# A two-layer hybrid attention trunk on one core: the last 512 output columns cut at 384 in place of 256, their last sum of squares on VectorE, and another list of issue

## The chip, the core and the metric

The kernel runs on one core of one Trainium2 chip. The metric is the device time of one execution in microseconds (us); three runs of the kernel before took 294.9, 294.93 and 295.31 us, median 294.93 us. A core has five engines, each of which executes its own instructions in the order in which they were put into its queue: TensorE (PE: matrix products; PEld is its loading of the stationary operand), VectorE (DVE), ScalarE (ACT), GpSimd (POOL) and SyncE (SP, which here only starts transfers). The engines wait for each other by semaphores. SBUF is the memory on the core, 128 partitions wide; PSUM is the memory in 8 banks into which TensorE writes.

## The reference

The input x is one sequence of 256 tokens with D = 1024 features, in 32-bit floats. Two layers follow one another, and a last normalization:

```
c_act = silu(c)
for layer in range(2):
    shift, scale, gate = split(c_act @ w_ada[layer] + b_ada[layer], 3)
    h = rms_norm(x, norm_g[layer]) * (1 + scale) + shift
    if layer == 0: y = even_mixer(h, ...)   # projections, attention A and B, w_out_even
    else:          y = odd_mixer(h, ...)    # projections, attention C, w_out_odd
    x = x + gate * y
return rms_norm(x, final_g)     # x * rsqrt(mean(x*x) + eps) * final_g
```

The even layer has two groups of 8 heads. Group A attends to a sliding window of 128 tokens with a learned sink for each head. Group B has three branches (compressed, selected and sliding window), each with a gate. The odd layer has 16 heads with causal attention in blocks of 256, which at 256 tokens is plain causal attention. In both, a SiLU path multiplies the heads' output before one output projection of 1024 x 1024.

## The kernel before, in words

**Products in three parts.** A 32-bit product is made of three products in a faster type. Each weight tile `raw` is split into a rounded part `whi` (a copy by ScalarE) and a remainder `wlo` (a subtraction by VectorE), each activation into `hhi`, `hlo` or `ghi`, `glo`, and `mm3` (L567) issues hi x hi, hi x lo and lo x hi into one bank. In the output projections the tokens are stationary, 128 at a time, and up to 512 weight columns stream past them: 8 slices of the inner dimension times 3 parts, 24 matmuls for 128 tokens and one bank. Each of these matmuls loads its own 128 x 128 stationary operand.

**Tokens.** The 256 tokens lie as two halves `t` = 0 and 1 of 128 partitions; `xs` (128 x 2 x 1024) holds the running x.

**Attention.** `quad_probs` (L1023) handles four heads. TensorE writes the scores into four banks; for each head VectorE adds the mask and takes the minimum (`tensor_tensor_reduce`), ScalarE takes the exponential, VectorE the reciprocal of the sum; the multiplication by it is split between VectorE and ScalarE. Then TensorE transposes the head's probabilities, tile `sm`, in three matmuls of 128 columns with the identity (a part of the tile `ta`) into the bank `ps_pt`, of which there is one, and ScalarE copies the bank into `pT`:

```
L37    BANKS = {"pj": 3, "s": 2, "pt": 1, "o": 1, "m": 1}
...
            pt = bank("pt")
            for n in range(3):
                T.transpose(pt[:, n * P : (n + 1) * P], sms[j][:, n * P : (n + 1) * P], ident)
            pT = sb([P, 3 * P], "pT", 4)
            A.copy(pT, pt[:, : 3 * P])
```

`quad_values` and `b_half` (L1102) then multiply `pT` with the values into the bank `ps_o`. In the traces `sm_125` to `sm_129` are the five buffers of `sm`, and slices of `bigA` serve as further ones.

**The junction.** The even layer's last attention is the second `b_half`; its output projection `out_proj` (L1179 to L1192) comes next. Since the projection's first products need only heads that are finished, its matmuls (`ps_pj` from `whi`, `wlo` and `ghi`, `glo`, 512 columns) stand in TensorE's queue between the transposes of that last attention. Between them stand the conditioning's small products for the odd layer (bank `ps_m`; `acc` is their sum, made by VectorE).

**The end.** The odd layer's output projection (L1244 to L1279) runs by halves of 512 output columns `n`. In the second half the gate is multiplied into the raw weights first, so that the product can be added to `xs` without it. Within a half the work goes by pieces, each a bank of its own: token half 0 with 512 columns, then token half 1, which for n = 1 is in two pieces of 256 columns (L1259). `plan.fence("pe")` keeps TensorE's pieces in this order. After each piece `add_scaled` (L377) adds the bank to `xs` on VectorE and sums the squares of those columns, then VectorE multiplies them by the final weights `fg` into `ot` (a view of the tile `oT`). The square goes to ScalarE, whose sum goes to a column of `parts`; GpSimd adds the sums of a token half's earlier pieces into another column of it. After the last piece of a token half ScalarE takes the root of the sum (with the earlier pieces' sum as its bias), VectorE the reciprocal, and ScalarE scales columns 0 to 320 (`CUT`) of `ot` and VectorE the other 704; a transfer of each follows.

**What sets the order.** Nothing is issued while the program above runs: every call is recorded by `Plan` (L178 to L260) with the earlier calls it depends on. At the end `Plan.issue` goes through the table `ORDER` (L38), 2985 numbers of recorded calls, and issues them in that order, each to its own engine's queue. The table can put any call anywhere as long as what it depends on stands ahead of it. Since all are issued from one line, every instruction of the trace has the line L252 (L253 in the changed kernel), and one tells them apart by their tiles.

The transfers of the weights go through SP's queue into five buffers `raw`; some small loads at the start go through ScalarE's and GpSimd's queues.

Of the kernel before, what the change touches and what calls it, by code (L numbers as in the profile page):

```python
# [38 lines left out]
0 4 74 8 10 3 5 11 2 12 9 6 13 1 14 15 7 77 16 17 34 18 35 59 75 79 22 19 76 36 20 60 78 38 61 80 39 30 42 62 63  # L39
21 64 37 65 81 66 67 69 70 44 45 71 72 46 47 48 83 82 96 97 98 99 100 101 102 103 104 105 106 107 108 109 110  # L40
111 112 113 114 115 116 117 118 119 120 121 122 123 124 125 126 127 54 73 31 49 84 55 128 50 43 40 142 129 51 68
56 130 131 52 138 91 53 94 93 57 143 139 135 172 169 132 173 136 140 160 144 178 86 58 163 133 164 89 145 156
181 95 154 161 170 175 134 137 85 149 152 146 176 166 87 32 150 182 88 157 179 90 174 147 171 177 141 151 148
153 196 92 162 208 209 180 219 158 222 165 23 167 183 255 202 205 203 210 184 187 159 211 223 199 212 224 193
220 194 168 197 225 190 206 198 188 221 191 226 227 228 229 230 231 232 233 234 235 236 237 238 239 240 241 242
243 244 245 214 155 246 213 256 189 207 185 247 248 204 253 200 201 25 192 195 216 186 215 249 250 264 257 260
286 254 277 268 278 269 251 259 252 330 289 290 291 258 217 262 218 266 274 331 271 287 261 283 288 279 272 273
263 316 280 281 313 310 317 284 301 282 270 318 295 267 285 304 328 292 302 332 327 311 307 333 319 275 305 329
296 320 303 276 334 297 335 306 265 321 298 314 336 337 338 339 340 341 342 343 344 345 346 347 357 358 322 293
308 348 349 309 355 350 324 351 323 352 315 294 299 353 354 300 325 359 356 312 370 361 391 388 392 389 366 326  # L50
379 393 418 373 371 360 382 364 419 362 385 390 376 420 377 368 424 365 374 363 369 383 415 384 378 386 425 416
380 426 427 421 428 412 375 400 406 429 372 381 367 397 413 422 387 409 401 451 402 394 403 423 398 399 404 407
405 430 431 432 433 434 435 436 437 438 439 440 441 452 442 395 414 443 444 449 445 447 446 516 417 410 517 453
512 455 396 450 408 411 833 458 464 456 485 482 462 448 473 646 474 467 483 454 476 470 484 486 479 459 460 475
468 702 465 466 487 469 488 480 546 457 489 461 471 506 463 491 547 490 518 521 492 493 477 509 472 519 494 478
515 520 510 481 523 550 507 522 551 553 525 524 495 554 500 552 555 559 497 496 536 556 535 534 508 557 558 498
501 562 832 548 537 647 499 560 549 605 563 511 502 527 561 565 566 567 604 836 532 564 530 571 526 568 603 569
543 572 606 573 538 570 574 575 533 577 578 704 576 579 580 703 583 584 585 531 513 708 581 582 589 503 542 648
539 607 608 609 618 705 610 612 619 586 587 711 712 620 529 709 710 714 590 504 591 713 595 588 505 623 831 611
596 592 593 621 717 715 716 594 540 706 720 541 721 597 718 649 622 719 624 722 723 726 724 639 626 640 613 625  # L60
614 707 615 616 650 641 727 728 725 729 730 627 732 731 733 734 738 735 514 739 617 736 27 628 644 629 602 630
28 651 834 643 906 598 631 737 26 740 741 744 742 745 743 528 633 599 747 41 642 601 600 746 750 860 632 840 748
907 749 753 751 752 754 755 634 635 756 757 545 636 652 655 544 637 653 838 656 839 858 24 654 657 1057 835 658
638 758 759 760 761 762 763 764 765 766 767 768 769 770 771 772 773 776 782 837 778 777 783 843 844 842 841 847
848 846 845 851 852 850 849 855 856 854 853 659 784 786 1065 908 774 661 775 662 660 785 859 780 788 792 779 909
968 969 970 971 972 973 974 975 976 977 978 979 980 981 982 983 793 910 864 861 863 862 868 865 867 866 872 869
871 870 876 873 875 874 986 781 663 664 790 787 665 789 791 984 667 1066 668 666 994 995 990 991 877 794 996 670
29 795 671 878 992 797 985 803 879 796 912 998 880 881 798 1002 987 799 669 673 674 675 679 800 680 814 672 681
911 882 913 988 685 676 809 883 808 677 989 686 678 1000 682 884 1001 683 1067 801 687 691 802 1003 692 693 885
684 688 689 690 1068 886 694 804 805 697 914 695 806 698 696 887 807 699 1069 888 889 890 891 892 893 894 895  # L70
896 897 898 899 900 901 902 903 700 1132 1133 1134 1135 1136 1137 1138 1139 915 701 810 918 919 1070 904 999 921
815 920 997 811 812 1140 993 905 1004 1148 916 1071 924 922 925 1041 1042 1043 1044 926 813 1005 923 1142 930
1006 1255 927 928 816 817 1045 1013 929 1007 818 1256 933 1072 1146 931 932 819 1150 934 935 1012 939 1046 1047
1008 936 937 917 940 1048 1144 938 1257 1025 1049 941 1147 1141 942 945 1009 1010 943 946 947 944 951 1018 948
1050 949 950 1011 1262 1152 1051 1077 952 953 954 1014 1015 1258 1019 1016 1052 1143 1053 1154 955 957 958 1145
1259 1024 1054 1076 1078 1260 956 959 1153 1017 960 961 963 1149 964 1194 1195 1196 1197 1198 1199 1200 1201
1401 1020 1079 962 1208 965 1055 1210 1273 1151 966 1021 1261 1022 1056 967 1023 1058 1155 820 821 822 823 824
825 826 827 1156 1026 1211 1027 1028 1082 1059 1085 1209 1157 1029 1086 1159 1087 1091 1083 1092 1212 1080 1084
1093 1402 1060 1170 1088 1164 1061 1062 1171 1089 1090 1097 1094 1214 1098 1063 1095 1099 1263 1206 1064 1103
1202 1073 1216 1272 1104 1213 1158 1096 1165 1100 1105 1160 1264 1207 1204 1265 1161 1162 1163 1101 1102 1106  # L80
1107 1081 1205 1278 1279 1280 1281 1282 1283 1284 1285 1217 1166 1203 1266 1167 1215 645 1168 1108 1109 1176
1169 1438 1112 1292 1113 1114 1267 1118 1119 1110 1177 1172 828 1173 1218 1174 1290 1293 1175 1111 1268 1115
1030 1031 1032 1033 1034 1035 1036 1037 1219 1274 1178 1221 1179 1116 1180 1294 1117 1220 1120 1288 1226 1181
1121 1275 1124 1122 857 1222 1227 1233 1223 1125 1296 1300 1286 1224 1276 1298 1126 33 1123 1127 1225 1277 1128
1295 829 1437 1074 1075 1228 1229 1230 1289 1129 1130 1232 1340 1341 1342 1343 1344 1345 1346 1347 1403 1416
1269 1038 1231 1443 1234 1287 1444 1299 1239 1235 1404 1297 1238 1301 1270 1291 1236 1405 1182 1183 1184 1185
1186 1187 1188 1189 1190 1191 1192 1193 1237 1240 1241 1271 1242 1039 1480 1406 1407 1408 1409 1410 1302 1131
1243 1411 1303 1244 1245 1246 1247 1248 1249 1250 1251 1305 1360 1304 1494 1362 1481 1311 1412 830 1488 1363
1306 1310 1307 1495 1356 1308 1354 1482 1309 1352 1489 1490 1491 1316 1357 1492 1312 1322 1313 1314 1496 1317
1497 1417 1418 1483 1040 1350 1348 1315 1498 1499 1506 1493 1353 1318 1422 1358 1319 1446 1320 1419 1500 1252  # L90
1323 1321 1501 1355 1502 1503 1361 1359 1420 1507 1324 1508 1504 1509 1351 1349 1505 1364 1421 1510 1511 1365
1325 1414 1562 1566 1413 1366 1423 1567 1326 1327 1328 1329 1330 1331 1332 1333 1334 1335 1336 1337 1338 1339
1424 1372 1367 1379 1445 1253 1368 1369 1425 1373 1378 1384 1370 1598 1599 1426 1574 1575 1371 1484 1374 1375
1376 1576 1577 1377 1254 1447 1427 1600 1518 1380 1381 1382 1601 1512 1385 1602 1383 1578 1386 1387 1486 1388
1485 1563 1487 1389 1448 1462 1428 1429 1430 1431 1432 1390 1391 1392 1393 1394 1395 1396 1397 1433 1398 1439
1603 1564 1568 1579 1463 1399 1513 1519 1440 1434 1520 1580 1514 1521 1522 1515 1441 1565 1516 1604 1400 1569
1517 1524 1525 1523 1530 1581 1442 1531 1435 1465 1449 1464 1526 1582 1532 1436 1527 1605 1528 1606 1533 1529
1570 1607 1536 1583 1534 1584 1535 1450 1685 1571 1608 1451 1572 1585 1452 1586 1587 1554 1453 1454 1455 1456
1573 1588 1589 1686 1537 1609 1538 1590 1558 1457 1555 1591 1592 1593 1458 1594 1595 1596 1597 1559 1610 1611
1556 1622 1612 1613 1614 1689 1415 1459 1539 1615 1616 1560 1623 1557 1624 1690 1691 1628 1617 1460 1618 1619  # L100
1620 1629 1631 1621 1625 1630 1466 1467 1468 1469 1470 1471 1472 1473 1632 1633 1626 1634 1461 1635 1561 1474
# [1247 lines left out]
```

## Time and profile before

| | before |
|---|---|
| median of three runs | 294.93 us (294.9 to 295.31) |
| profiled execution, first to last instruction | 292.6 us |
| TensorE busy | 281.4 us (96%) |
| VectorE busy | 248.8 us (85%) |
| ScalarE busy | 196.4 us (67%) |
| GpSimd busy | 9.1 us (3%) |
| bytes moved | 71.70 MB, mean 245 GB/s |
| mean granted TensorE clock | 0.987 |

The profile is of one execution. Its span of 292.6 us runs from the first instruction to the last one; the median of the runs has 2.3 us more than that, which lie before and behind, so a span is compared with spans and a run with runs. The clock is the share of full speed that TensorE was granted. In the rows by instruction the columns are the start in us, the duration, the engine, the operation and what it writes and reads, and in brackets the wait before it and who ended it. In the rows by group they are the count, the busy time, the mean duration in ns and, behind the bar, the idle time of the engine ahead of the group. A matmul's duration in such a row is longer than its share of TensorE's time, since successive ones overlap: the pace is read from start to start.

### The profile page before, as it was taken

The page shows a single profiled execution, that of the slowest core. Times are in us where ns is not written, and L with a number is a line of the kernel's source. Part 1 is how long each engine was busy: PE and PEld are TensorE (multiplying, and loading weights), DVE is VectorE, ACT ScalarE, POOL GpSimd, SP SyncE. Part 2 cuts the span into 40 slices and gives each one's busy share as a digit, 9 for nine tenths or more (in the row PEclk, how much of TensorE's full clock was granted, in tenths as well). Part 3 has the DMA queues.
Part 4 walks back from the last instruction along what each step waited for, and adds up shares of the span by engine and source line. Part 5 has one row for each costly group of instructions (what it writes and reads, how often), then busy time and mean ns, then how long its engine had stood idle before and what let it go on. Part 6 is the DMA issues. An engine that isn't in the chain of part 4 may idle for free.

```text
span 292.6 us, 6200 instructions
## 1 busy us (share of the span) xinstructions
PE 281.4 (96%) x2292; PEld 242.6 (83%) x2292; DVE 248.8 (85%) x585; ACT 196.4 (67%) x465; POOL 9.1 (3%) x34
## 2 busy tenths in 40 slices
PE   6899999999999999999999999999999999999991
PEld 5778887999799887777768899998899989887890
DVE  0398898999999999999999659898938899899963
ACT  3586356586999999995289652665459358793831
POOL 3200000000000000000010000000000000000100
PEclk9799999999999999999999999999999999999997
DMA  7999999998898849857969968965094874402003
GB/s 241 374 390 382 376 388 380 327 333 253 276 343 264 281 131 331 288 203 241 273 206 349 350 221 276 333 228 171 15 338 154 296 280 146 143 2 72 1 2 143
DMA packets 62398, 71.70 MB, mean 245 GB/s; under 512 B 3416, under 2 KB 53024, under 8 KB 62368
## 3 DMA queue, kind: packets, MB, share of 16 engines
q1 hardware_dynamic: 61792, 70.84, 72.9%
q10 hardware_dynamic: 448, 0.41, 0.4%
q8 instruction: 18, 0.29, 0.4%
q14 instruction: 12, 0.10, 0.1%
q0 software_dynamic: 128, 0.05, 0.1%
HBM read 70.25 MB, written 1.05 MB: 244 GB/s over the span
## 4 chain that ended last, share of the span: by engine, by line
PE 87%; DVE 7%; DMA 2%; ACT 2%; issue 1%; POOL 0%; DVEq 0%; ACTq 0%; POOLq 0%
PE ps_pj L252 56%; PE ps_s L252 11%; PE ps_o L252 8%; PE ps_pt L252 7%; PE ps_m L252 5%; DMA rows<-in_norm_g_dram 2%; DVE acc L252 1%; DVE sm L252 1%; DVE bigA L252 1%; DVE t L252 1%; DVE oT L252 1%; DVE wlo L252 1%; ACT whi L252 1%; ACT sm L252 0%; ACT hhi L252 0%
## 5 line engine op out<-in xcount | busy, mean ns | idle before, releaser
L252 ACT CAST whi<-raw 128x1024 fp32r<-128x1024 f32 (+4 forms) x84 | 75.4, 915 | 43.2 <-PE ps_pj L252 20.4
L252 DVE TENSOR_TENSOR wlo<-raw,whi 128x1024 fp32r<-128x1024 f32 (+4 forms) x84 | 87.5, 1057 | 11.2 <-ACT whi L252 11.1
L252 PE MATMUL ps_pj<-hhi,whi 128*128 128x256 f32 x272 | 66.6, 284 | 0.0
L252 PE MATMUL ps_pj<-hlo,whi 128*128 128x256 f32 x272 | 66.5, 286 | 0.0
L252 PE MATMUL ps_pj<-hhi,wlo 128*128 128x256 f32 x272 | 65.2, 284 | 0.0
L252 PEld LDWEIGHTS ps_pj<-hlo,whi 128*128 128x128 f32 x272 | 47.3, 188 | 0.9 <-issue 0.7
L252 PEld LDWEIGHTS ps_pj<-hhi,whi 128*128 128x128 f32 x272 | 47.7, 188 | 0.5 <-ACT bigA L252 0.2
L252 PEld LDWEIGHTS ps_pj<-hhi,wlo 128*128 128x128 f32 x272 | 47.1, 188 | 1.0 <-issue 0.8
L252 DVE SCALAR_TENSOR_TENSOR acc<-raw,cz,acc 128x512 f32<-128x512 f32 x49 | 36.5, 745 | 0.1
L252 ACT ACTIVATE sm<-sm,mn 128x256 f32<-128x256 f32 (+1 forms) x58 | 26.0, 449 | 5.3 <-DVE mn L252 5.2
L252 PE MATMUL ps_pj<-wlo,hhi 128*128 128x512 f32 (+1 forms) x56 | 21.2, 396 | 0.0
L252 PE MATMUL ps_pj<-whi,hlo 128*128 128x512 f32 (+1 forms) x56 | 21.1, 393 | 0.0
L252 PE MATMUL ps_pj<-whi,hhi 128*128 128x512 f32 (+1 forms) x56 | 20.7, 394 | 0.1
L252 PE MATMUL ps_pj<-whi,ghi 128*128 128x512 f32 (+1 forms) x56 | 20.5, 369 | 0.0
L252 PE MATMUL ps_pj<-whi,glo 128*128 128x512 f32 (+1 forms) x56 | 20.5, 367 | 0.0
L252 PE MATMUL ps_pj<-wlo,ghi 128*128 128x512 f32 (+1 forms) x56 | 20.3, 367 | 0.0
L252 PE MATMUL ps_pt<-ta,sm 128*128 128x128 f32 x87 | 15.8, 278 | 0.0
L252 ACT COPY pT<-ps_pt 128x384 f32<-128x384 f32 x25 | 11.8, 474 | 5.6 <-PE ps_pt L252 5.2
L252 DVE TENSOR_TENSOR t<-ps_pj,tF 128x512 f32<-128x512 f32 x18 | 11.8, 686 | 3.5 <-PE ps_pj L252 3.5
L252 ACT ACTIVATE t<-xs 128x512 f32<-128x512 f32 (+2 forms) x11 | 7.3, 665 | 9.2 <-DVE xs L252 7.7
L252 PEld LDWEIGHTS ps_pt<-ta,sm 128*128 128x128 f32 x87 | 10.5, 140 | 3.4 <-issue 1.7
L252 PEld LDWEIGHTS ps_pj<-whi,hhi 128*128 128x128 f32 x56 | 10.4, 188 | 2.7 <-ACT hhi L252 1.1
(251 smaller groups left out, 588.8 us busy)
## 6 DMA issues: line engine op xcount, KB each, us to landing
raw<-in_w_in_odd_dram SPq DMA_DIRECT2D x32, 512.0 KB, 5.9
raw<-in_w_ada_dram SPq DMA_DIRECT2D x28, 512.0 KB, 5.8
raw<-in_w_in_even_dram SPq DMA_DIRECT2D x10, 512.0 KB, 7.5
t<-in_w_ada_dram SPq DMA_DIRECT2D x16, 256.0 KB, 5.6
raw<-in_w_out_even_dram SPq DMA_DIRECT2D x8, 512.0 KB, 4.7
raw<-in_w_out_odd_dram SPq DMA_DIRECT2D x8, 512.0 KB, 4.3
raw<-in_w_in_even_dram SPq DMA_DIRECT2D x8, 396.0 KB, 6.0
qT<-in_w_ada_dram SPq DMA_DIRECT2D x12, 256.0 KB, 6.1
```

The lines of the kernel that those rows point to most:

```text
L252: self.ops.append(dict(key=eng.key, deps=deps, fn=lambda: getattr(real, name)(*args, **kw)))
```

## The change

There are three edits. The last two pieces of token half 1 are 384 and 128 columns wide where both had 256. The last piece's sum of squares is one instruction of VectorE, which multiplies the columns by themselves, scales by 1/D and adds them up, where ScalarE squared and summed; token half 0 keeps ScalarE's. And `ORDER` is another permutation of the same 2985 calls; of its numbers the diff here shows the first and the last line.

```diff
 ORDER = [int(i) for i in """
-0 4 74 8 10 3 5 11 2 12 9 6 13 1 14 15 7 77 16 17 34 18 35 59 75 79 22 19 76 36 20 60 78 38 61 80 39 30 42 62 63
...
-2968 2969 2970 2971 2972 2920 2950 2973 2921 2974 2975 2976 2978 2922 2977 2979 2980 2923 2981 2983 2982 2984
+2 8 10 11 12 13 14 15 16 17 18 19 20 21 23 22 0 1 3 75 80 74 77 76 30 26 32 25 5 29 4 28 7 59 60 61 24 6 62 78
...
 """.split()]
@@ add_scaled
         V.tensor_tensor(xs[:, t, cs], py if scaled else yt, xs[:, t, cs], ALU.add)
-        if last and scaled:
+        if last and scaled and t == 1:
+            V.tensor_tensor_reduce(out=yt, in0=xs[:, t, cs], in1=xs[:, t, cs], scale=1.0 / D, scalar=0.0, op0=ALU.mult, op1=ALU.add, accum_out=part[:, 1:2])
+        elif last and scaled:
             A.activation(yt, xs[:, t, cs], AF.Square, scale=D**-0.5, accum_out=part[:, 1:2])
@@ final projection
-        pieces = ((0, 0, 512), (1, 0, 512)) if n == 0 else ((0, 0, 512), (1, 0, 256), (1, 256, 512))
+        pieces = ((0, 0, 512), (1, 0, 512)) if n == 0 else ((0, 0, 512), (1, 0, 384), (1, 384, 512))
```

The first place is TensorE's queue at the junction, where the last attention's transposes (`ps_pt` from `sm`) meet the output projection (`ps_pj`). A row is one instruction, or several alike with their count; its columns are the line, the operation, what it writes and reads, and its size. Before:

```order
L252 MATMUL ps_o_97<-pT_132,vb 64x128
L252 MATMUL ps_pj_94<-whi_109,ghi 128x512
L252 MATMUL ps_m_67<-ta,asb_108 128x128
L252 MATMUL ps_pj_93<-whi_109,ghi 128x512
L252 MATMUL ps_pt_84<-ta,sm_126 128x128 x2
L252 MATMUL ps_pj_94<-wlo_113,ghi 128x512
L252 MATMUL ps_pt_84<-ta,sm_126 128x128
L252 MATMUL ps_pj_93<-wlo_113,ghi 128x512
L252 MATMUL ps_pj_93<-whi_109,glo 128x512
L252 MATMUL ps_pj_93<-whi_109,ghi 128x512
L252 MATMUL ps_pj_93<-wlo_113,ghi 128x512
L252 MATMUL ps_pt_84<-ta,sm_127 128x128 x3
```

And in the changed kernel:

```order
L253 MATMUL ps_o_97<-pT_132,vb 64x128
L253 MATMUL ps_pt_84<-ta,sm_126 128x128 x3
L253 MATMUL ps_pt_84<-ta,sm_127 128x128 x3
L253 MATMUL ps_m_67<-acc_106,ones 32x128 x4
L253 MATMUL ps_pt_84<-ta,sm_128 128x128
L253 MATMUL ps_m_67<-ta,asb_108 128x128
L253 MATMUL ps_pt_84<-ta,sm_128 128x128 x2
L253 MATMUL ps_pj_94<-whi_109,ghi 128x512
L253 MATMUL ps_pj_94<-wlo_113,ghi 128x512
L253 MATMUL ps_pt_84<-ta,sm_129 128x128 x2
L253 MATMUL ps_pj_94<-whi_109,glo 128x512
```

Matmuls of the projection that stood between two heads' groups of transposes now stand behind them; between the groups of `sm_126` and `sm_127` nothing is left, and behind the latter stand four small products of the conditioning.

The second place is VectorE's queue at the end of the run, from the multiplication by `fg` of token half 0's last columns on. Before:

```order
L252 TENSOR_TENSOR oT<-xs,bigA 128x512
L252 TENSOR_TENSOR xs<-ps_pj_94,xs 128x256
L252 TENSOR_TENSOR oT<-xs,bigA 128x256
L252 TENSOR_SCALAR oT<-oT,parts 128x704
L252 RECIPROCAL parts<-parts 128x1
L252 TENSOR_SCALAR oT<-oT,parts 128x704
```

And in the changed kernel, from the reciprocal of token half 0 on; the row `ISA t_89` is the new sum of squares, the one below it the read of its sum:

```order
L253 RECIPROCAL parts<-parts 128x1
L253 TENSOR_SCALAR oT<-oT,parts 128x704
L253 TENSOR_TENSOR xs<-ps_pj_93,xs 128x384
L253 TENSOR_TENSOR oT<-xs,bigA 128x384
L253 TENSOR_TENSOR xs<-ps_pj_94,xs 128x128
L253 ISA t_89,parts<-xs 128x128
L253 ISA parts 128x1
L253 RECIPROCAL parts<-parts 128x1
L253 TENSOR_TENSOR oT<-xs,bigA 128x128
L253 TENSOR_SCALAR oT<-oT,parts 128x704
```

Token half 0's scaling moved ahead of the 384-column piece's add, and the last multiplication by `fg` stands behind the last reciprocal where it stood ahead of it.

248 rows, old and new, of the table ORDER are left out of this document.

## The prediction

> **What bounds the kernel now.** I read the page first (busy times, then the chain that ended last), then the busy times by stretch, then the waits of TensorE, and last the end of the run instruction by instruction.
>
> ```profile
> span 292.6 us, 6200 instructions
> PE 281.4 (96%) x2292; PEld 242.6 (83%) x2292; DVE 248.8 (85%) x585; ACT 196.4 (67%) x465; POOL 9.1 (3%) x34
> PE 87%; DVE 7%; DMA 2%; ACT 2%; issue 1%; POOL 0%; DVEq 0%; ACTq 0%; POOLq 0%
> ...
> 15.60:95.00 79.40, 79.30 (x701) 68.51 (x701) 74.76 (x187) 56.60 (x149) 1.17 (x8) 1.00 0.99 337
> 95.00:130.00 35.00, 34.91 (x288) 27.44 (x287) 34.66 (x112) 34.74 (x103) 0.00 (x0) 1.00 0.73 241
> 130.00:280.20 150.20, 150.09 (x1151) 131.23 (x1150) 130.30 (x262) 94.03 (x190) 2.63 (x5) 1.00 0.63 204
> 280.20:286.10 5.90, 5.90 (x50) 5.67 (x48) 3.31 (x7) 2.30 (x8) 0.56 (x2) 1.00 0.07 24
> 286.10:292.60 6.50, 0.02 (x1) 0.00 (x0) 2.10 (x5) 1.37 (x4) 0.00 (x0) 0.69 0.37 140
> ...
> PE ps_o L252 <- ACT hhi L252: 0.6, 1, 0.6
> ```
>
> The rows by stretch give the stretch, its length, and the busy time of TensorE, its weight loads, VectorE, ScalarE and GpSimd. Three things are to be seen. From 15.6 us to 286.1 us TensorE is busy in all but 0.3 us; the last row is the only one of the waits of TensorE over this stretch, 0.6 us at its very beginning, where the first projection waits for its input. So the list of issue has almost nothing left to win there, and whatever adds to TensorE's time adds to the run. Between 95 and 130 us VectorE and ScalarE are as full as TensorE: in this stretch a wait that appears is not made good by an engine that had time to spare. After 286.1 us only VectorE, ScalarE and the output's transfer are left, 6.5 us.
>
> **The tail, TensorE's part.** The second half of the tokens gets its last 512 output columns in two pieces of 24 matmuls, 256 columns wide. They become 24 of 384 and 24 of 128 columns.
>
> ```profile
> 280.04 0.40 PE L252 MATMUL ps_pj<-whi,glo 128*128 128x512 f32 x1
> 280.27 0.28 PE L252 MATMUL ps_pj<-whi,ghi 128*128 128x256 f32 x1
> 280.39 0.28 PE L252 MATMUL ps_pj<-wlo,ghi 128*128 128x256 f32 x1
> ...
> 285.84 0.27 PE L252 MATMUL ps_pj<-whi,glo 128*128 128x256 f32 x1
> ```
>
> From start to start a matmul of 512 columns takes 0.23 us and one of 256 takes (285.84 - 280.27)/47 = 0.1185 us, so at these widths the columns set the pace, 0.463 ns each. 24 matmuls of 384 columns then take 24 x 0.178 = 4.27 us. For 128 columns the trace of before has no such row. By the columns alone it would be 0.059 us, 1.42 us for the 24. But each of these matmuls has a weight load of its own, which the narrower matmul does not shrink:
>
> ```profile
> L252 PEld LDWEIGHTS ps_pj<-whi,ghi 128*128 128x128 f32 x56 | 10.5, 188 | 1.8 <-issue 0.3
> L252 PEld LDWEIGHTS ps_o<-pT,vb 128*64 128x64 f32 x60 | 4.9, 136 | 1.8 <-issue 0.4
> L252 PEld LDWEIGHTS ps_m<-t,cz 128*32 128x32 f32 x48 | 1.2, 109 | 0.6 <-DMA raw<-in_w_in_even_dram 0.3 <-issue 0.3
> ...
> 1.05 3.78 PE L252 MATMUL ps_m<-ones 128*128 128x128 f32 x16 [1.05 <-DVE ones L252]
> ```
>
> A load of 32, 64 and 128 columns takes 109, 136 and 188 ns: (188 - 109)/96 = 0.82 ns for each column and a latency that can overlap with the load before. At 0.82 ns a load of 128 columns fills 0.105 us, which hides under a matmul of 256 columns (0.1185 us) and not under one of 128 (0.059 us). I take 0.105 us: 24 x 0.105 = 2.52 us. Before: 48 x 0.1185 = 5.69 us. After: 4.27 + 2.52 = 6.79 us. TensorE ends **1.10 us later**. Bounds: 0.059 us each gives 4.27 + 1.42 = 5.69, no change. The dearest passes of 128 columns in the trace are those of the warm-up, 16 in 3.78 us or about 0.22 us each; at that price the 24 take 5.3 us and TensorE ends 3.9 us later.
>
> The Trainium skill, "TensorE: Matmul & The Clock Gate", section "LDWEIGHTS (loading the stationary operand)", gives a load its columns over 1.2 ns, 107 ns for 128, which the slope of 0.82 ns above agrees with. The same page's section "Back-to-back issue gap" has about 81 ns for a stream of load and matmul pairs at 128 columns; by that, as an estimate, the 24 would take 1.94 us and TensorE would end 0.5 us later instead of 1.1. No row here shows such a pair at 128 columns in this type.
>
> **The tail, behind the last matmul.** The last piece's add, square, root, reciprocal and scaling:
>
> ```profile
> 286.15 0.42 DVE L252 TENSOR_TENSOR xs<-ps_pj,xs 128x256 f32<-128x256 f32 x1 [0.81 <-PE ps_pj L252]
> 286.61 0.43 DVE L252 TENSOR_TENSOR oT<-xs,bigA 128x256 f32<-128x256 f32 x1
> 286.67 0.42 ACT L252 ACTIVATE t<-xs 128x256 f32<-128x256 f32 x1 [1.87 <-DVE xs L252]
> 286.96 0.58 DVE L252 TENSOR_SCALAR oT<-oT,parts 128x704 f32<-128x704 f32 x1
> 287.00 0.19 ACT L252 ACTIVATION_READ_ACCUMULATOR t<-xs 128x1 f32 x1
> 287.21 0.29 ACT L252 ACTIVATE parts<-parts 128x1 f32<-128x1 f32 x1
> 287.54 0.16 DVE L252 RECIPROCAL parts<-parts 128x1 f32<-128x1 f32 x1
> 287.74 0.59 DVE L252 TENSOR_SCALAR oT<-oT,parts 128x704 f32<-128x704 f32 x1
> ...
> L252 DVE TENSOR_TENSOR xs<-ps_pj,xs 128x512 f32<-128x512 f32 x1 | 0.7, 692 | 0.7 <-PE ps_pj L252 0.7
> L252 DVE CUSTOM_DVE_ANT_0 sm<-ps_s,tb 128x128 f32<-128x128 f32 x11 | 3.1, 282 | 1.2 <-PE ps_m L252 1.2
> L252 DVE DVE_READ_ACCUMULATOR2_ANT mn<- 128x1 f32 x80 | 6.7, 83 | 0.0
> ```
>
> Now: from 286.15 to 287.74 + 0.59 = 288.33, 2.18 us. After: the add at 128 columns, 0.42 less half of the step from 256 to 512 columns, (0.69 - 0.42)/2: 0.29. The sum of squares on VectorE is the same kind of instruction as the softmax's masked minimum, 0.28 at 128 columns, and the read of its sum, which overlaps it but for some 0.01: 0.29, in place of 0.42 + 0.19 on ScalarE less their overlap and the hop of 0.10 before them. The root is 0.29 and the reciprocal 0.16 as now. New in the way: VectorE's list has the multiplication by the final weights behind the reciprocal, where now it runs while ScalarE squares; at 128 columns it is 0.30 by the same step, with the 0.08 by which one VectorE instruction begins inside another. Then the scaling, 0.59. With five hops of 0.03 to 0.04: 0.29 + 0.29 + 0.29 + 0.16 + 0.22 + 0.59 + 0.16 = 2.00 us. That is **0.18 us saved**; between 0.0 (the new sum costs 0.18 more) and 0.5 (the multiplication hidden as now). The square of the 384 columns on ScalarE and GpSimd's addition of it end before they are wanted: about 0.55 for the add, 0.75 for the square with its read, 0.4 for GpSimd and hops, 1.8 us from the piece's end, while TensorE still has 2.5 us to go and the root comes 0.65 us later; with 0.059 us a matmul it would just fit, 1.4 + 0.65. The first half's root is wanted earlier on VectorE: its reciprocal and scaling now stand ahead of the add of the 384 columns, and would hold it up if the root came late. It comes at 282.3 us (the row below), with 0.2 and 0.6 behind it 283.1 us, and the 384 columns are not done before 280.27 + 4.27 = 284.5 us.
>
> ```profile
> 282.01 0.30 ACT L252 ACTIVATE parts<-parts 128x1 f32<-128x1 f32 x1
> ```
>
> Tail together: +1.10 - 0.18 = **+0.9 us**.
>
> **The list of issue.** It moves instructions everywhere. Where TensorE transposes softmax rows there is one bank, ps_pt, and a group of three transposes cannot follow another until ScalarE has copied the bank out.
>
> ```profile
> L252 PE MATMUL ps_pt<-ta,sm x16: 270/272/328, 108.4 to 124.3; 128*128 128x128 f32 x16
> L252 ACT COPY pT<-ps_pt x4: 462/474/481, 112.6 to 120.4; 128x384 f32<-128x384 f32 x4
> ...
> 65.89 0.60 PE L252 MATMUL ps_pt<-ta,bigA 128*128 128x128 f32 x4
> ...
> L252 ACT ACTIVATE sm<-sm,rc 128x256 f32<-128x256 f32 x9 | 4.5, 511 | 0.0
> ```
>
> From the start of the third transpose: 0.27 to its end, 0.47 for the copy and two hops of 0.04, 0.82 us; the transpose itself holds TensorE for (0.60 - 0.27)/3 = 0.11. So 0.71 us of other matmuls must stand between two groups or TensorE waits. At 110 to 120 us, where the even layer's last attention runs into its output projection, the list of before has four to six matmuls of 512 columns between groups, at 0.23 us each enough. The new list has two (0.47), none, four small ones (0.36) and two (0.47): short by 0.24, 0.71, 0.35 and 0.24, in all **1.5 us**, in the one stretch where ScalarE and VectorE are full and cannot run ahead. Other groups in the new list have their cover. Bounds: nothing, if the waits displace gaps that are in TensorE's row now; 3.5 us, if ScalarE in each case first ends one of the 0.51 us rows that stand in its queue (four times 0.5 more).
>
> What the new list may win: the 0.6 us above, and gaps too small to be listed. The start does not move by more. Ten transfers, two of x and eight of the conditioning weights, stand first on SP's queue in both lists, x now ahead of all, and the first projection needs them all. GpSimd's small loads now stand behind its clears, and the last of them behind the row that waits for x:
>
> ```profile
> 7.21 0.56 POOL L252 TENSOR_TENSOR r<-r,expo 128x1 f32<-128x1 f32 x1 [3.73 <-DVE r L252]
> 13.16 0.61 PE L252 MATMUL ps_m<-gate,cz 128*32 128x128 f32 x16
> ...
> rows_pe<-in_cmp_pe_k_dram POOLq DMA_DIRECT2D x1, 8.0 KB, 5.6
> ```
>
> Issued at 7.8 us and 5.6 us under way it lands at 13.4 us; TensorE now wants it behind the last conditioning matmuls, which start at 13.2 us and take 0.6. So it is just hidden, and if x's lead does not bring that row forward it could cost some tenths. I take 0.5 us won, between -0.5 and 1.
>
> Sum against the profiled run: 292.6 + 0.9 + 1.5 - 0.5 = 294.5 us. The median of the runs, 294.93 us, lies 2.3 us above that span, for what precedes the first instruction and follows the last; so **296.8 us**.
>
> **The rivals.** *Wide and narrow cost alike by the column, and the list is harmless.* For it: at 256, 512 columns the pace is that of the columns, and a load can begin while an earlier one ends. Against it: the load's 0.82 ns. Then the tail is -0.2 and the list -0.5: 294.2 us, faster. It decides from a pace below 0.09 us at 128 columns together with no waits at ps_pt. *Both small.* The narrow matmuls cost 0.08 to 0.1 us and the waits at ps_pt take the place of gaps that exist: within 0.6 us of 294.9. *Narrow matmuls fall to the price of the warm-up's passes*, 0.22 us: for it, that no matmul of the split weights in this trace is narrower than 256 columns, so that nothing shows they keep their pace; against it, that the warm-up is in the first microseconds, and transposes of the same 128 columns take 0.11 us at 65.89 us, half of it. Then +3.9 - 0.2 + 1.5 - 0.5: 299.6 us.
>
> **How the numbers follow.** A measurement of this kernel tells about 0.2%, 0.6 us, from no change. The forecast, +0.6 to +3.5, has 0.47; the price of the warm-up 0.14; both small 0.16; the faster rival 0.23. So slower 0.61, the same 0.16, faster 0.23. The likeliest case's own range is 295.6 to 298.4. The faster rival's far end is both gains at their bounds, -0.5 behind the last matmul and -1.0 by the list: 293.4 us. The range for 8 in 10 takes in most of it and most of the dear case: 293.7 to 299.6.
>
> **What would show it.** In the new profile: the start-to-start time of the 128-column matmuls, 0.105 us forecast, 0.06 or 0.22 by the rivals; TensorE's last matmul about 2.1 us later than 286.1, of which 1.1 lies behind the start of the 384-column piece; waits of TensorE for ScalarE's copies out of ps_pt between 105 and 120 us; and 2.0 us from the last add's start to the end of the last scaling. The forecast is wrong if the last matmul ends by 286.5 us, or if the waits at ps_pt are there and the end has not moved.

## The result

The changed kernel takes 296.93 us, median of five runs (296.65 to 298.1), against 294.93 us, also the median of five (294.63 to 295.7): a ratio of 1.0066, interval 1.0044 to 1.0087, so 0.4 to 0.9% slower. The forecast was 296.8 us. One more set of runs on another occasion gave 1.0089 (1.0070 to 1.0108). The profiled execution spans 295.0 us, 2.4 us more than before.

The profile page of the changed kernel, span and busy times:

```profile
span 295.0 us, 6204 instructions
PE 283.7 (96%) x2292; PEld 242.7 (82%) x2292; DVE 250.5 (85%) x587; ACT 197.1 (67%) x463; POOL 9.2 (3%) x34
```

TensorE is as full as before, 96%, and its 2.3 us more of busy time are nearly the 2.4 us of the span. Its busy time does not tell a narrow matmul that takes longer per column from useful work, and since a row lasts longer than its pace, it hides the first tenths of a gap. The waits of TensorE from 15.6 us on tell more:

```profile
PE ps_pt L253 <- DVE sm L253: 0.8, 1, 0.8
PE ps_pj L253 <- ACT whi L253: 0.4, 1, 0.4
PE ps_pj L253 <- DVE wlo L253: 0.4, 1, 0.4
PE ps_s L253 <- ACT kTb L253: 0.3, 1, 0.3
PE ps_pj L253 <- DVE t L253: 0.2, 1, 0.2
```

Where before had one wait, 0.6 us at the very start, there are now five, and the longest is that of a transpose into ps_pt for softmax rows of VectorE.

**Where the 2.4 us lie.** I laid the two rows of TensorE side by side at equal work done, each matmul counted at the usual start-to-start time of its shape. The changed kernel is 0.6 us ahead at 40 us, 0.9 us ahead at 117 us, 1.3 us behind at 124 us, 1.9 us behind at 130 us, and still 1.9 us behind where the last two pieces begin (282.15 us against 280.27). So the junction of the even layer's last attention and its output projection costs 2.8 us within thirteen, 2.2 of them in the first seven, and from there to the tail nothing of note happens. The junction in the changed kernel, by instruction (start, duration, engine, operation, and in brackets a wait and its releaser):

```profile
117.72 0.55 PE L253 MATMUL ps_pt<-ta,sm 128*128 128x128 f32 x3
119.02 0.52 PE L253 MATMUL ps_pt<-ta,sm 128*128 128x128 f32 x3 [0.76 <-DVE sm L253]
119.59 0.43 PE L253 MATMUL ps_m<-acc,ones 128*32 128x128 f32 x8
120.16 0.33 PE L253 MATMUL ps_pt<-ta,sm 128*128 128x128 f32 x1
...
121.54 0.51 PE L253 MATMUL ps_pj<-wlo,ghi 128*128 128x512 f32 x1 [0.35 <-DVE wlo L253]
...
118.59 0.28 DVE L253 TENSOR_SCALAR sm<-sm,rc 128x128 f32<-128x128 f32 x1
...
118.30 0.48 ACT L253 COPY pT<-ps_pt 128x384 f32<-128x384 f32 x1 [0.24 <-PE ps_pt L253]
118.68 1.05 ACT L253 CAST whi<-raw 128x1024 fp32r<-128x1024 f32 x1
119.62 0.48 ACT L253 COPY bigA<-ps_pt 128x384 f32<-128x384 f32 x1
```

The second group of transposes, at 119.02 us, comes 0.9 us later than it would behind a free bank. Two things end almost together ahead of it: ScalarE's copy of the bank (118.30 + 0.48 = 118.78 us) and VectorE's multiplication of the rows (118.59 + 0.28 = 118.87 us). The third group, at 120.16 us, waits for a copy that ScalarE began at 119.62 us: the second group's transposes had ended just before, at 119.02 + 0.52 = 119.54 us, and the rounding of a weight tile ahead of the copy was ending too. At 121.54 us a projection matmul waits for a remainder `wlo` that VectorE got to late. A last part is no wait: the 24 products into `ps_o` from 124.86 us on take 2.77 us, where the same 24 took 2.34 from 126.12 us on before. The last eight, of 128 columns, started about every 0.05 us before and start about every 0.11 us in the new order; why was not traced.

VectorE has lost time well ahead of this. Its busy time (the third figure behind the commas, after TensorE and its loads) between 62 and 85 us and between 85 and 116 us, in the kernel before:

```profile
62.00:85.00 23.00, 23.00 (x260) 20.35 (x258) 22.86 (x73) 18.72 (x60) 1.17 (x8) 1.00 0.91 293
85.00:116.00 31.00, 30.91 (x304) 25.60 (x304) 31.00 (x106) 30.73 (x97) 0.00 (x0) 1.00 0.79 257
```

And in the changed kernel:

```profile
62.00:85.00 23.00, 22.74 (x285) 19.77 (x284) 21.90 (x67) 18.75 (x58) 1.24 (x8) 1.00 0.99 320
85.00:116.00 31.00, 30.90 (x280) 25.36 (x276) 29.57 (x106) 30.78 (x99) 0.00 (x0) 1.00 0.70 224
```

The longest of its waits between 62 and 130 us, two of them together:

```profile
DVE rc L253 <- ACT sm L253: 1.1, 2, 0.8
```

Before, VectorE had no gap at all in the 31 us ahead of the junction; now it works 22.86 + 31.00 - 21.90 - 29.57 = 2.4 us less in these two stretches, and 1.1 us of that is two reciprocals that stand at the head of its queue while ScalarE still works at the exponentials.

**The tail of the changed kernel**: the first matmul of 384 columns, the second and the last of 128, and what follows:

```profile
282.15 0.34 PE L253 MATMUL ps_pj<-whi,ghi 128*128 128x384 f32 x1
...
286.38 0.27 PE L253 MATMUL ps_pj<-wlo,ghi 128*128 128x128 f32 x1
...
288.84 0.27 PE L253 MATMUL ps_pj<-whi,glo 128*128 128x128 f32 x1
...
289.15 0.29 DVE L253 TENSOR_TENSOR xs<-ps_pj,xs 128x128 f32<-128x128 f32 x1 [1.47 <-PE ps_pj L253]
289.59 0.29 DVE L253 CUSTOM_DVE_ANT_0 t<-xs 128x128 f32<-128x128 f32 x1
...
290.25 0.17 DVE L253 RECIPROCAL parts<-parts 128x1 f32<-128x1 f32 x1 [0.36 <-ACT parts L253]
290.33 0.27 DVE L253 TENSOR_TENSOR oT<-xs,bigA 128x128 f32<-128x128 f32 x1
290.64 0.59 DVE L253 TENSOR_SCALAR oT<-oT,parts 128x704 f32<-128x704 f32 x1
```

The 128-column matmuls follow one another at (288.84 - 286.38)/22 = 0.112 us. From the first start to the last the two pieces take 6.69 us, where they took 285.84 - 280.27 = 5.57: +1.12 us. From the last add to the end of the last scaling it is 2.08 us, where it was 2.18. The end of the span comes 295.0 - 291.23 = 3.8 us behind that, where it came 4.2 us behind (at 292.56 us, the last scaling's end at 288.33). The issue of the output's transfers on SP's queue shows a reason, in the kernel before and in the changed one:

```profile
287.56 1.14 SPq L252 DMA_DIRECT2D out_dram<-oT  x2
```

```profile
285.39 6.20 SPq L253 DMA_DIRECT2D out_dram<-oT  x2
```

Each row is the two transfers of SP's queue together. Before, token half 0's part left 0.8 us ahead of the last one; now it leaves at 285.4 us, and beside the last one, behind 291.2 us, only ScalarE's smaller part is under way. So the span's 2.4 us are -0.9 + 2.8 + 1.1 - 0.1 - 0.5.

### The profile page after: what moved, and what is told of

Read it like the earlier page. It is cut to its first block, busy times and chain, and to the rows that moved or that the text cites. A ratio compares the mean times of both kernels' runs of the same rounds, so it can differ in the third digit from the quotient of the medians.

```text
span 295.0 us, 6204 instructions
## 1 busy us (share of the span) xinstructions
PE 283.7 (96%) x2292; PEld 242.7 (82%) x2292; DVE 250.5 (85%) x587; ACT 197.1 (67%) x463; POOL 9.2 (3%) x34
## 4 chain that ended last, share of the span: by engine, by line
PE 81%; ACT 8%; DMA 5%; DVE 3%; SPq 1%; issue 1%; DVEq 0%
PE ps_pj L253 56%; PE ps_s L253 11%; PE ps_pt L253 5%; PE ps_o L253 5%; PE ps_m L253 4%; ACT sm L253 3%; DMA raw<-in_w_in_even_dram 3%; ACT bigA L253 2%; DMA qT<-in_w_ada_dram 2%; SPq L253 1%; DVE acc L253 1%; DVE t L253 0%; DVE oT L253 0%; ACT pT L253 0%; ACT acc L253 0%
## 5 line engine op out<-in xcount | busy, mean ns | idle before, releaser
L253 PE MATMUL ps_pj<-hhi,whi 128*128 128x256 f32 x272 | 71.4, 288 | 0.0
L253 PE MATMUL ps_pj<-hhi,wlo 128*128 128x256 f32 x272 | 71.1, 286 | 0.0
L253 PE MATMUL ps_pj<-hlo,whi 128*128 128x256 f32 x272 | 70.6, 287 | 0.0
L253 PEld LDWEIGHTS ps_pj<-hlo,whi 128*128 128x128 f32 x272 | 48.7, 188 | 1.0 <-issue 0.7
L253 PEld LDWEIGHTS ps_pj<-hhi,wlo 128*128 128x128 f32 x272 | 49.2, 188 | 0.3
L253 ACT ACTIVATE sm<-sm,mn 128x128 f32<-128x128 f32 (+1 forms) x58 | 25.9, 449 | 4.6 <-DVE mn L253 4.6
L253 PE MATMUL ps_pj<-wlo,ghi 128*128 128x512 f32 (+2 forms) x56 | 20.5, 375 | 0.4 <-DVE wlo L253 0.4
L253 PE MATMUL ps_pj<-whi,ghi 128*128 128x512 f32 (+2 forms) x56 | 20.8, 377 | 0.0
L253 PE MATMUL ps_pj<-whi,glo 128*128 128x512 f32 (+2 forms) x56 | 20.7, 373 | 0.0
L253 PE MATMUL ps_pt<-ta,sm 128*128 128x128 f32 x87 | 17.6, 277 | 1.0 <-DVE sm L253 0.8
```

The lines of the kernel that those rows point to most:

```text
L253: self.ops.append(dict(key=eng.key, deps=deps, fn=lambda: getattr(real, name)(*args, **kw)))
```

## The experiments

New and old list mean the two tables `ORDER`. Since the numbers of both stand for the same calls, the first n of one can be followed by all others in the order of the other; where their positions agree except for a few calls, such a seam changes little else. In the diffs `old` and `new` stand for these numbers.

### Each part alone

**The list alone.**

```diff
-ORDER = old
+ORDER = new        # code of before: 256 and 256 columns, ScalarE's square
```

> The kernel before (256 and 256 columns, ScalarE's square) with the whole new list of issue. The prediction's terms give +1.5 us where TensorE waits at the junction of the even layer's last attention and its output projection, -0.5 us elsewhere, and none of the +1.1 us of the narrow matmuls: about 295.9 us, +1.0 us over the kernel before. The profile of the changed kernel, read before this run, has TensorE 0.9 us ahead of before at 117 us and 1.9 us behind at 126 us: by that +1.9 us, 296.8 us. The rival that the narrow piece alone carries the loss: within 0.3 us of before.

Measured: 297.87 us against 295.18, ratio 1.0092 (1.0062 to 1.0121). The list costs time without the narrow piece, and more than either expectation had. The size is not settled by this kernel: its runs lie between 296.9 and 299.8 us, apart from one at 350.64, and the profiled one is from the upper end, with a mean granted clock of 0.938. The even pieces below, the same list with VectorE's sum of squares, come out lower.

**The tail alone.**

```diff
-ORDER = new
+ORDER = old[:2900] + rest in the order of new        # code of the change
```

> The changed code (384 and 128 columns, the sum on VectorE), with the list of before up to its first 2900 numbers, that is to the last projection pieces, and the new list's order for the last 85. The prediction gives +0.9 us (+1.1 us of TensorE, -0.18 us behind it): 295.8 us. The matmuls of 128 columns should follow one another at 0.105 to 0.112 us. The rival that the columns alone set the pace gives -0.2 us: 294.7 us. The rival that the junction carries all of the loss also gives at most +0.2 us.

Measured: 295.73 us against 295.18, ratio 1.0026 (1.0010 to 1.0041): +0.3 to +1.2 us. Its trace has the first 384-column matmul, the last of 128 columns and the last scaling at

```profile
280.72 0.34 PE L248 MATMUL ps_pj<-whi,ghi 128*128 128x384 f32 x1
287.40 0.27 PE L248 MATMUL ps_pj<-whi,glo 128*128 128x128 f32 x1
...
287.71 0.29 DVE L248 TENSOR_TENSOR xs<-ps_pj,xs 128x128 f32<-128x128 f32 x1 [1.48 <-PE ps_pj L248]
...
289.20 0.59 DVE L248 TENSOR_SCALAR oT<-oT,parts 128x704 f32<-128x704 f32 x1
```

6.68 us for the two pieces (+1.11), 2.08 us behind the last matmul (-0.10), and 3.8 us to the end of its span of 293.6 us (-0.4): +0.6 us, which the timing bears out. The forecast of +0.9 us lies within the interval, but it lacked the earlier transfer.

**The new list's first 110 us alone.**

```diff
-ORDER = old
+ORDER = new[:1250] + rest in the order of old        # code of before
```

> The kernel before, with the new list's first 1250 numbers (to about 110 us) and all others in the order of before. The prediction has -0.5 us for what the new list wins, without a place: 294.4 us. The profile of the changed kernel says that 0.6 to 0.9 us are won before 110 us; if the old list behind it keeps them, 294.1 us, -0.8 us. The rival: what is won in the first 110 us is given back at the next wait for VectorE or ScalarE, which do not run ahead with TensorE: within 0.3 us of before.

Measured: 295.88 us, ratio 1.0030 (1.0015 to 1.0046), slower: neither expectation. TensorE's row is 1.0 us ahead of before at 109 us, 1.0 us behind at 115 us and 1.2 us behind at 120 us, though the order there is again the old one. In it VectorE has gaps of 2.3 us between 65 and 115 us where the kernel before had 0.1. From 105 us on TensorE waits 1.0 us in all for VectorE and 0.9 us for ScalarE's copies out of ps_pt, so VectorE's lateness is not the seam's only cost.

**The junction's 201 operations alone.**

```diff
-ORDER = old
+ORDER = old[:1250] + rest of new[:1450] + rest in the order of old        # code of before
```

> The kernel before, with the new list's order only for the 201 operations between about 110 and 130 us (the list of before for the first 1250 numbers, then what the new list has among its first 1450, then the order of before). The prediction's term gives +1.5 us: 296.4 us. The new profile's loss between 117 and 126 us is 2.8 us, of which 0.9 us had been won ahead: if VectorE and ScalarE set the time at this place whatever TensorE won before, +1.9 us, 296.8 us; if the whole loss is the order's own, +2.8 us, 297.7 us. The rival that the waits displace other gaps: within 0.3 us of before.

Measured: 298.94 us, ratio 1.0127 (1.0103 to 1.0151), +3.8 us, the dearest of all and above every expectation. Its waits of TensorE:

```profile
PE ps_o L248 <- DVE oT L248: 1.3, 1, 1.3
PE ps_pt L248 <- ACT pT L248: 0.6, 1, 0.6
PE ps_pt L248 <- ACT bigA L248: 0.4, 1, 0.4
```

The first comes right behind the seam and belongs to it, since VectorE's old order had put that row later. The other two are what the prediction named: ScalarE's copies out of ps_pt (`bigA` is the other tile they go to), between transposes that stand too close. The three sum to 2.3 us; TensorE's row loses 4.1 us from 110 to 130 us, and where the rest lies was not traced. So either half of the new list's first 130 us loses time here in company with the old other half; their losses, 0.9 and 3.8 us, do not add up to that of the whole list. That the waits lie beside one another and a seam adds its own would explain it, but was not shown.

### Who sets the time ahead of the junction

**Two more instructions of VectorE at 101 us**, and the same at 164 us:

```diff
             self.ops[i]["inst"] = self.ops[i]["fn"]()
+            if i == 1263:        # 1683 in the second kernel
+                for _ in range(2):
+                    self.extra()
...
+    plan.extra = lambda: tc.nc.vector.tensor_tensor(scr, xs[:, 0, 0:512], xs[:, 0, 512:1024], ALU.mult)
```

> The kernel before, with two more instructions of VectorE at 101 us, each a product of two stretches of 512 columns of x into a tile that nobody reads, 0.60 to 0.67 us each from start to start. If VectorE sets the time between 70 and 125 us: 1.2 to 1.3 us over the kernel before. If TensorE does and VectorE has as much to spare there as its 85% over the whole run says: no change, within 0.3 us.

> The kernel before with the same two more instructions of VectorE as at 101 us, which cost 0.9 us there, now at 164 us, where VectorE has gaps of 1.1 and 2.1 us in the next six. If it is the missing slack between 70 and 125 us that makes VectorE's time count, they cost nothing here, within 0.3 us. If any instruction more on VectorE, or the kernel's other layout of memory, costs: 0.5 to 0.9 us again.

Measured: 295.8 against 294.9 us at 101 us, ratio 1.0034 (1.0018 to 1.0050); 295.47 against 295.22 us at 164 us, ratio 1.0000 (0.9983 to 1.0017). The two instructions in VectorE's row of the first kernel:

```profile
101.32 1.40 DVE L1281 TENSOR_TENSOR scr<-xs 128x512 f32<-128x512 f32 x2
```

And the one wait of TensorE in it between 80 and 135 us:

```profile
PE ps_pt L248 <- DVE sm L248: 0.9, 1, 0.9
```

VectorE's next instruction starts 1.3 us later, TensorE waits for it once, 0.9 us, for softmax rows, and the run is 0.5 to 1.5 us longer. At 164 us the same two cost nothing, within 0.5 us. VectorE is at 85% over the whole run; what counted here is that it has no gap between 75 and 125 us.

**VectorE's waits filled.** In the changed kernel, four calls that are ready are put ahead of the two waiting reciprocals on VectorE:

```diff
-... 1264 1218 1176 1219 1265 1220 1266 ...
+... 1264 1265 1176 1218 1219 1220 1266 ...
-... 1276 1302 1238 1303 1277 1304 1403 ...
+... 1276 1238 1277 1302 1303 1304 1403 ...
```

> The changed kernel, with four numbers of its list moved on VectorE alone: at 106.0 and 114.6 us, where VectorE stands in front of a reciprocal that waits for ScalarE's exponentials (0.75 and 0.33 us), a conditioning sum and a multiplication that are ready and stand behind it are put ahead of it. TensorE's and ScalarE's orders stay. If VectorE's waits between 70 and 116 us carry the loss at the junction, 0.9 to 1.0 us of it come back: 1.0 us under the changed kernel. The prediction's reason, transposes that stand back to back in TensorE's order and wait for ScalarE's copies, gives no change, within 0.3 us of the changed kernel.

> The changed kernel once more, on the chip of the three others, to compare them with it: 1.0 us over the kernel before at least and 2.6 us at most by the interval of its first runs. The new list with the old last pieces came out at 2.7 us over before, which leaves nothing for the narrow matmuls; if that was the new list's own spread, this run shows more than 2.0 us, if not it shows 2.0 us again and the list alone and the list with the narrow piece cost alike.

Measured: 297.29 us (ratio 1.0086, 1.0067 to 1.0106) against 297.41 us for the changed kernel beside it: no difference. (The changed kernel itself is 2.5 us over before here, 2.0 us in its first runs, so the loss differs between occasions.) In the trace VectorE's gaps from 65 to 120 us fell from 2.5 to 1.6 us, and TensorE no longer waits for it at the junction. What TensorE waits for instead, between 105 and 135 us:

```profile
PE ps_pt L248 <- ACT pT L248: 0.6, 1, 0.6
PE ps_pt L248 <- ACT bigA L248: 0.4, 1, 0.4
```

At 124 us TensorE is 0.4 us better off than in the changed kernel, at 135 us only 0.1 us. So my theory that VectorE's waits carried the loss falls as it stood: they are one of two causes that cover each other. With VectorE on time, the transposes that stand back to back wait for ScalarE's copies, as the prediction had it. The gap ahead of the second group shrinks only from 0.9 to 0.7 us, so at this wait the copy sets most of it and VectorE's lateness adds 0.2 us. No run has TensorE's old order at the junction inside the new list: its projection matmuls need banks and weight tiles that ScalarE and VectorE free and fill later in the new list.

**The new list to 70 us, the old one behind it.**

```diff
-ORDER = old
+ORDER = new[:725] + rest in the order of old        # code of before
```

> The kernel before, with the new list's first 725 numbers (to about 70 us, where five operations of GpSimd are all that the new list has issued and the old one has not) and the order of before behind them. The first runs made a new theory: between 70 and 125 us VectorE sets the time, since in the kernel before it has no gap there at all, and each microsecond in which it waits there is lost. By it the new list's first 70 us are a gain, since VectorE has 1.0 to 1.5 us less of waits behind it there, and the old order behind them keeps it: 0.6 to 1.2 us under the kernel before. The rival, that the profiles of the first 30 us differ by up to 1 us between executions of one list and the new list has no lead at all: within 0.3 us of before.

Measured: 294.1 us against 294.9, ratio 0.9982 (0.9968 to 0.9997): 0.1 to 0.9 us under the kernel before, and so below both. Its runs lie between 293.8 and 294.68 us, those of before beside it between 293.64 and 295.68: its best is no better, what it lacks are the late ones. The seam at 70 us leaves VectorE's old order from there on, its gaps from 75 to 125 us sum to 0.1 us, and TensorE's loss at the junction is gone: it stays 0.3 us ahead of before from 85 us to the end. At 68 us it is 1.0 us ahead; the other 0.7 us go between 68 and 85 us.

### What a narrow matmul costs

**Half the weight load.** The tail alone, and in it 18 of the last 24 matmuls take 64 tokens as stationary operand; their products for the other 64 tokens are left out.

```diff
-mm3(py[:, : c1 - c0], ghi[:, k, sl], glo[:, k, sl], ...)
+pe_, sk = (HD, slice(t * P, t * P + HD)) if c0 == 384 and 0 < k < KT - 1 else (P, sl)        # HD is 64
+mm3(py[:pe_, : c1 - c0], ghi[:, k, sk], glo[:, k, sk], ...)
```

> The kernel with the changed tail and the old list ahead of it (0.3% over before in its own run), in which 18 of the last piece's 24 matmuls take as stationary operand 64 tokens in place of 128, so that each weight load is half as wide and the moving columns stay 128. It leaves out those products for the last 64 tokens. If the weight load's columns set the pace of 0.112 us, these 18 go at 0.055 to 0.06 us, 0.9 us less of TensorE: TensorE ends 0.9 to 1.0 us earlier than in that kernel. If each matmul has a fixed cost of issue that no width shrinks: the same 0.112 us.

Measured: 295.0 us, ratio 0.9986 (0.9970 to 1.0002): 1.2 us under the tail alone by the ratios, 0.7 us by the medians. First and last of the 18:

```profile
285.67 0.22 PE L248 MATMUL ps_pj<-whi,ghi 128*64 128x128 f32 x1
...
286.69 0.22 PE L248 MATMUL ps_pj<-whi,glo 128*64 128x128 f32 x1
```

1.02/17 = 0.060 us each, where the same 128 moving columns behind a load of 128 took 0.112. That is 18 x 0.052 = 0.9 us less of TensorE. The load's width set the pace, not a fixed cost of issue; at 0.060 the pace is that of the columns again, 128 x 0.463 ns = 0.059 us.

**448 and 64 columns.**

```diff
-((0, 0, 512), (1, 0, 384), (1, 384, 512))
+((0, 0, 512), (1, 0, 448), (1, 448, 512))        # the tail alone
```

> The same kernel with the last pieces at 448 and 64 columns. If the weight load sets the pace below 240 columns, the 24 matmuls of 64 columns take 0.112 us each as those of 128 do, and TensorE's two pieces take 24 x 0.207 + 24 x 0.112 = 7.7 us, 0.7 us more than with 384 and 128; the add, the sum and the multiplication behind the last matmul are shorter by 0.07 us each at most: 0.5 to 0.7 us over that kernel. If the columns set the pace: 5.7 us for the two pieces, as in the kernel before, and the time at or below it.

Measured: 296.42 us, ratio 1.0042 (1.0022 to 1.0062), about 0.5 us over the tail alone (1.0026). The second and the last matmul of 64 columns:

```profile
286.05 0.27 PE L248 MATMUL ps_pj<-wlo,ghi 128*128 128x64 f32 x1
288.50 0.28 PE L248 MATMUL ps_pj<-whi,glo 128*128 128x64 f32 x1
```

(288.50 - 286.05)/22 = 0.111 us for half the columns: the pace no longer falls. At 0.463 ns a column the two costs meet at 112/0.463, about 240 columns, so by this estimate 256 is close to the narrowest piece that costs TensorE nothing.

**256 and 256 columns in the changed kernel.**

```diff
-((0, 0, 512), (1, 0, 384), (1, 384, 512))
+((0, 0, 512), (1, 0, 256), (1, 256, 512))        # the new list, the sum on VectorE
```

> The changed kernel, its list and its sum on VectorE, with the last two pieces at 256 columns each again. By the traces TensorE's last two pieces are then 1.2 us shorter, and behind the last matmul the add, the sum and the multiplication by the final weights 0.13 us longer each: 0.8 to 1.1 us under the changed kernel, so 1.0 to 1.7 us over the kernel before. The rival, from the runs so far, in which the new list with the old pieces was no faster than the changed kernel: no change against it, 2.0 to 2.5 us over the kernel before.

Measured: 296.23 us, ratio 1.0040 (1.0021 to 1.0059), against 1.0066 and 1.0089 for the changed kernel: 0.8 to 1.4 us less. Its trace:

```profile
282.35 0.28 PE L248 MATMUL ps_pj<-whi,ghi 128*128 128x256 f32 x1
287.90 0.27 PE L248 MATMUL ps_pj<-whi,glo 128*128 128x256 f32 x1
...
288.21 0.42 DVE L248 TENSOR_TENSOR xs<-ps_pj,xs 128x256 f32<-128x256 f32 x1 [1.86 <-PE ps_pj L248]
...
290.10 0.59 DVE L248 TENSOR_SCALAR oT<-oT,parts 128x704 f32<-128x704 f32 x1
```

The two pieces take 5.55 us again (-1.14 against the changed kernel). From the last add to the end of the last scaling it is 290.10 + 0.59 - 288.21 = 2.48 us, 0.4 us longer than with 128 columns and 0.3 us longer than in the kernel before. The list alone, with the same order of VectorE and ScalarE's square, takes 2.51 us there: at 256 columns VectorE's sum wins next to nothing over ScalarE's square, and the multiplication by the final weights behind the reciprocal costs the 0.3 us. Against the changed kernel it is -0.7 us together.

## Why the prediction was right

| term of the sum | forecast | measured in the trace |
|---|---|---|
| TensorE's last two pieces | +1.10 us | +1.12 us; +1.11 in the tail alone |
| chain behind the last matmul | -0.18 us | -0.10 us |
| the output's transfer | not in the sum | -0.5 us |
| waits at the junction | +1.5 us | +2.8 us, 0.4 of it slower products and no wait |
| what the list wins | -0.5 us | -0.9 us by 117 us |
| span | +1.9 us | +2.4 us |
| time of a run less its span | 2.3 us | 1.8 us |

The time came out within 0.2 us of the forecast; the terms that make it up did not all come out so well, and errors of both signs cancelled. That it came so close is luck. The last matmul started 3.0 us later than before (288.84 against 285.84 us) where 2.1 was forecast; 0.5 us came back in the transfer, and 0.5 us in the step from span to run. I took the 2.3 us between the median and the profiled span as a fixed piece, but in every run here that has both figures the time is 1.73 to 1.86 us over the span. The rest of the 2.3 is that the execution profiled before was a short one: at 1.8 us over its span it would be a run of 294.4 us, as an estimate.

**The narrow matmuls** are the step that held best. 0.105 us was taken for 128 columns, 0.112 was measured. The step that gave it, that the weight load's columns fill a time which the narrower matmul cannot hide, is shown by the two runs that change one of the two widths: half the load brings the pace to 0.060 us, half the moving columns leaves it at 0.111. The trace of before had the price in another type: its transposes, 128 columns behind a load of 128 of their own, go at the 0.11 us that the prediction read but, for this question, held only against its dearest rival. The Trainium skill, "TensorE: Matmul & The Clock Gate", gives a load its columns over 1.2 ns in its section "LDWEIGHTS (loading the stationary operand)", 107 ns for 128 columns, which agrees with 0.112, and about 81 ns for a stream of load and matmul pairs at 128 columns in "Back-to-back issue gap", which does not. The rival at the price of the warm-up's passes, 0.22 us, falls, and so does the one by the columns alone.

**Behind the last matmul**, 2.08 us against 2.00. Between the add's end, 289.44 us, and the sum of squares, 289.59 us, lie 0.15 us where I had put a hop of 0.03 to 0.04.

**The transfer** is the term that I did not have. The list moves token half 0's scaling and its transfer ahead of the last two adds; I noted it only as a risk for the add. The six profiles here with the old tail order have 4.2 to 4.4 us from the last scaling to the span's end, seven of the eight with the new one 3.7 to 3.9 us; the list alone, with 4.6, stands apart and speaks against it. That the shared way of the two transfers is the reason is argued from the times of issue; no run here changes that alone.

**The junction** was named at the right place, and its forecast mechanism is there: with VectorE's waits filled, the gaps at ps_pt are what is left, 0.73 us ahead of the second group (from 117.92 us, the last transpose before, to 118.76, less 0.11), where 0.71 was forecast, and a wait of 0.4 us ahead of the third, where 0.35 was. The two others, of 0.24 us each, show as no wait. But in the changed kernel itself the first of these waits is put down to VectorE, which comes 0.1 us behind the copy, and the term was undersized: the new list also leaves VectorE idle for 2.4 us on its way there, which I did not look for, though I had read from the rows by stretch that it had none to spare. The cost of an instruction at 101 us shows what that reading was worth.

**What the list wins.** Seven profiles of the old list's first 40 us lie 0.4 us before to 1.0 us behind the one shown, 0.4 us behind in the mean; six of seven of the new list's lie 0.5 to 0.7 us ahead of it, one 0.5 us behind. By the means of both the new list's start is about 0.9 us better, nearly twice what I took. The execution profiled before was 0.4 us better than its kind, which would account for what the span's +2.4 us has over the +2.0 us of the medians. Where the gain lies also tells against a reading of the prediction, that a row of TensorE idle for 0.3 us has almost nothing left to win: from 20 to 68 us the row of before is idle for 0.1 us, and the new list gains about 0.6 us on it there.

**Still open**: which of the moves between 70 and 110 us make VectorE late, and how the 2.8 us split between it, the copies and the slower products into `ps_o`, since the first two cover each other.

## What to carry to other kernels

Where several engines are full in the same stretch, time lost in any of their queues can be time lost for the run (here 1.3 us more of VectorE cost 0.9 us), and repairing one of two losses that cover each other shows next to nothing while the other stands: read the busy time of every engine by stretch, and look for instructions that wait at the head of a queue with ready work behind them. A last piece of 128 columns, narrower than the width at which the weight load takes as long as the matmul (here about 240 columns), cost TensorE 1.1 us and shortened what follows by 0.1 us. And a list of issue can be tested in parts: the first part of one followed by the other's rest told the good 70 us from the bad 60 behind them, and gave a kernel 0.1 to 0.9 us under the better of the two.

## What was unexpected of the hardware

A matmul of 64 moving columns behind a load of 128 takes 0.111 us, no less than one of 128 columns (0.112); behind a load of 64 columns, 128 moving columns take 0.060 us. The same two VectorE instructions cost 0.9 us at 101 us and nothing at 164 us. And the last transfer seems to end about 0.4 us sooner when the one ahead of it left several microseconds earlier and not 0.8, in seven of eight profiles.
